# A build-time model of all engines sets the order of the mixing stage; attention's loads one by one

## The chip, the cores and the metric

The kernel runs on one core of a Trainium2 chip. The core has TensorE (PE in the profile, its weight loads PEld), VectorE (DVE), ScalarE (ACT), GpSimd (POOL) and SyncE (SP), which only issues DMA transfers; ACT and POOL issue some as well. Each engine works through its own list of instructions in order and waits for the others by semaphores. The metric is the device time of one execution in microseconds.

## The reference

Two layers (DEPTH 2, width 1024) of a diffusion backbone over 128 context tokens and 512 latent tokens, which share the weights. In each layer:

```
h   = (x * (1 + scale1) + shift1) @ W_in
mix = W_out([ RWKV-7 (4 heads) | neighbourhood attention (4 heads) | GQA (8 q heads, 2 kv heads) ])
x   = LN1(alpha * x + gate1 * mix)
x   = LN2(alpha * x + gate2 * SwiGLU(x * (1 + scale2) + shift2))
```

RWKV is a linear recurrence, forwards and backwards, with a 64 x 64 state per head. In the neighbourhood attention a latent token (8 rows of 64) sees the 8 x 16 tokens around it, with a relative bias, and 256 cached context tokens. In GQA latent tokens see all 512 latent and 256 cached tokens. Context tokens see only each other. All data are fp32; the large products are made of three products of rounded halves.

## The kernel before, in words

A layer runs in stages: the projections with `W_in`, during which the RWKV features begin; `mixing` (L459 on), in which the recurrence and attention run side by side; `mixed`, the first tiles of `W_out`; `tail`, the rest of `W_out`, LN1, the SwiGLU and LN2. Mixing of layer 0 takes about 292 to 562 us of the span, that of layer 1 about 1338 to 1617 us.

The recurrence is done in chunks of 64 tokens, as eight jobs a layer (two pairs of heads, two halves, two directions) in two slots, so that two jobs are under way at a time. A job has these steps. The products FT,BK on PE (two heads and five chunks) give a matrix per chunk; ACT copies it to `X` (L716), and it is written to DRAM as `md` by a DMA that ACT issues (L720) and read back as `BT` in blocks of 16 x 16 by a DMA that POOL issues (L723). DVE inverts the blocks, with some twenty small instructions (L775 to L788). The inverse goes out as `xd` and `td` (L794, L793, issued by ACT) and comes back as `X` and `T` (L799, L797, issued by POOL), two DMAs each, one for each head. Then PE widens the inverse from blocks to chunks, beginning with T times A, and runs through the states S of the five chunks.

Attention is a list of units: six context pairs, then the neighbourhood group 0 (na0) in four units, na1 in four, and four groups of GQA (two kv heads with two halves of the query heads each) in four. A unit makes the scores of two heads on PE into a PSUM tile `ps_s2` (two of them exist), the softmax on DVE and ACT gives `prob`, PE transposes it (PSUM tag `rw`, three banks), and the product with the values goes to `ps_pv`, one bank for a whole group. Names: `qs` and `ks` are queries and keys as they lie for the scores, loaded by SP from DRAM copies (`nqd`, `nkd`, `gqd`, `gkd`); `vw` are the values of a neighbourhood group, eight DMAs from `vd`; `bias` is the relative bias of one head, four DMAs from `rpx` (L948), to which POOL adds a mask (L949). `gv`, `gvc`, `nvc` and `vc` are values of GQA and of the context.

The work is written as Python generators (tasks). Each `yield` gives a latency in us that the author puts for the step. `weave` (L267 to L272) takes the task that is ready first on a clock of its own, `te.now`, which only matmuls move forward. Two attention tasks share the list of units. What the tasks emit isn't the last word: a layer beneath orders each engine's list by priority, which is the order of emission, and by its own simulation, and places the buffers.

```
def weave(self, *tasks):
    while any(t in self.tasks for t in tasks or self.tasks):
        t = min(self.tasks, key=lambda t: (max(t.ready - self.te.now, 0.0), t.ready))
        self.te.now = max(self.te.now, t.ready)
        self.step(t)
```

Of the kernel before, what the change touches and what calls it, by code (L numbers as in the profile page):

```python
# [16 lines left out]
P = 128  # L17
# [12 lines left out]
CH = 64  # L30
# [46 lines left out]


class Task:
    def __init__(self, gen, rank=0):  # L80
        self.gen, self.rank, self.ready = gen, rank, 0.0


class Build:
    def __init__(self, tc, I, O):
        self.tc, self.nc, self.I, self.O = tc, tc.nc, I, O

    def t(self, shape, name, dt=F32):
# [153 lines left out]
    def spawn(self, gen, rank=0):  # L242
        t = Task(gen, rank)
        t.ready = self.te.now
        self.tasks.append(t)
        return t

    def step(self, t):
        lat = next(t.gen, self)
        if lat is self:  # L250
            self.tasks.remove(t)
        else:
            t.ready = self.te.now + (lat or 0.0)

    def tick(self):
# [11 lines left out]
    def weave(self, *tasks):  # L267

        while any(t in self.tasks for t in tasks or self.tasks):
            t = min(self.tasks, key=lambda t: (max(t.ready - self.te.now, 0.0), t.ready))  # L270
            self.te.now = max(self.te.now, t.ready)
            self.step(t)  # L272
# [10 lines left out]
    def psum(self, tag):  # L283

        bufs, n = {"s2": (2, 1024), "rw": (3, 512), "pv": (1, 512)}[tag]
        return self.pp_pool.tile([P, n], F32, name="ps_" + tag, tag="ps_" + tag, bufs=bufs)

# [174 lines left out]
    def mixing(self, l, op):  # L462
        self.op = op
        with self.tc.tile_pool(name=f"at{l}", bufs=2, side="right", reuse_waits="tile") as at:
            self.at = at
            self.load_attn(l)
            for k in range(2, KT):
                self.out[k] = op.tile([P, NT], F32, name=f"o{k}"),
            self.weave(*(self.spawn(self.attention(self.units_), 2) for _ in range(2)))

# [161 lines left out]
    def rwkv_job(self, l, ft, hb, d, slot, pool):  # L632
# [121 lines left out]
        def inverse():  # L754
# [43 lines left out]
            for h in range(2):  # L798
                nc.gpsimd.dma_start(J.X[hs[h]], self.mat(xdr, h))  # L799
            yield 1.5  # L800

# [119 lines left out]
    def load_attn(self, l):  # L921
        nc, I, at = self.nc, self.I, self.at
        self.nvc = at.tile([P, 2, 256], F32, name="nvc", bufs=1)
        nc.gpsimd.dma_start(self.nvc, I["c_na_v"][l])
        self.gvc = at.tile([P, 2, P], F32, name="gvc", bufs=1)
        self.units_ = self.units(l)
        first = next(self.units_)
        self.units_ = itertools.chain([first], self.units_)
        nc.gpsimd.dma_start(self.gvc, I["c_g_v"][l])

    def na_values(self, l, ft):

        nc = self.nc
        vw = self.at.tile([P, 4, 2, P], F32, name="vw", bufs=1)
        vr = self.vd.rearrange("(r c) f -> r c f", c=64)[:, :, ft * P:(ft + 1) * P]
        for j in range(4):
            for hf in range(2):
                nc.sync.dma_start(vw[:, j, hf, :], vr[hf * 4:hf * 4 + 4, NA_LO[j]:NA_LO[j] + NA_N, :])  # L938
        return vw

    def na_bias(self, l, hd):

        nc = self.nc
        bias = self.at.tile([P, 4, 8, NA_N], F32, name="bias", bufs=2)
        for j in range(4):
            b = self.rpx[0:1]
            off = hd * 15 * 16 * (RP - 1) + PAD + 15 + NA_LO[j] - 16 * j
            nc.sync.dma_start(bias[:, j], bass.AP(tensor=b.tensor, offset=b.offset + off, ap=[[RP - 1, P], [16 * (RP - 1), 8], [1, NA_N]]))  # L948
            nc.gpsimd.tensor_tensor(bias[:, j], bias[:, j], bc(self.nmask[:, j * NA_N:(j + 1) * NA_N], 1, 8), ALU.add)  # L949
        return bias  # L950

# [5 lines left out]

    def doubled(self, dram, h):

        t = self.at.tile([P, 2, 768], F32R, name="ks", tag="ks", bufs=3)  # L960
        for u in range(2):
            self.nc.sync.dma_start(self.r32(t[u * CH:(u + 1) * CH]), dram[:, h * CH:(h + 1) * CH, :].rearrange("a p n -> p a n"))
        return t

# [135 lines left out]
    def units(self, l):  # L1100
        def load(ft):
            bias = [self.na_bias(l, 2 * ft + h) for h in range(2)]
            vw, ks = self.na_values(l, ft), [self.doubled(self.nkd[ft], h) for h in range(2)]
            return vw, [(self.stacked(self.nqd[ft], h, "qs", NLAT, 4), ks[h], bias[h]) for h in range(2)]
        vw, qk = load(0)
        for kt in range(6):
            yield self.ctx_pair(l, kt)
        for ft in range(2):
            if ft:
                vw, qk = load(ft)  # L1110
            st = {}
            for j in range(4):
                yield self.na_pair(l, ft, j, qk, vw, st)
        for kv in range(2):
            ks = self.doubled(self.gkd, kv)
            for m in range(2):
                qs = [self.stacked(self.gqd[2 * m + u], kv, "qs", NLAT, 4) for u in range(2)]
                st = {}
                for t in range(4):
                    yield self.gqa_pair(l, kv, m, t, qs, ks, st)  # L1120

# [36 lines left out]
    def ctx_pair(self, l, kt):  # L1158
# [19 lines left out]
        for h in range(2):  # L1178
            pT.append(self.transposed(pr[h], 1))
            yield 0.8728 if h else 0.0  # L1180
        pv = self.psum("pv")
        for h in range(2):
# [11 lines left out]
    def na_pair(self, l, ft, j, qk, vw, st):  # L1194
# [5 lines left out]
        for h in range(2):  # L1200
# [9 lines left out]
            mx = self.tp.tile([P, 1], F32, name="mx", tag="mx", bufs=4)  # L1210
            nc.vector.tensor_tensor_reduce(ps[:, 0:nw], ps[:, 0:nw], bias[:, j].rearrange("p r n -> p (r n)"), 1.0, mc, ALU.add, ALU.max, mx)
            nm = self.tp.tile([P, 1], F32, name="nm", tag="nm", bufs=4)
            nc.vector.tensor_scalar(nm, mx, -1.0, None, ALU.mult)
            if j == h == 0:
                st["sm"] = self.tp.tile([P, 4, 2], F32, name="sms", tag="sms", bufs=2)
            pr.append(self.softmax(ps[:, 0:512], 512, nm, 1.0, st["sm"][:, j, h:h + 1]))
            yield 3.2729999999999997 if h else 0.0
        for h in range(2):
            pT.append(self.transposed(pr[h], 4))
            yield 1.091 if h else 0.0  # L1220
        if j == 0:
            st["pv"] = self.psum("pv")
        pv = st["pv"]
# [4 lines left out]
        if j == 3:  # L1228
# [3 lines left out]
            view = lambda t: t.rearrange("p (j r c) -> p j r c", j=4, r=8)  # L1232
            self.normed(o.rearrange("p (r j c) -> p j r c", r=8, j=4), pv, st["sm"], view)

    def gqa_pair(self, l, kv, m, t, qs, ks, st):
# [4 lines left out]
        for h in range(2):  # L1240
# [8 lines left out]
            nc.vector.tensor_tensor(nm, nm, sc, ALU.mult)  # L1249
            if t == h == 0:  # L1250
                st["sm"] = self.tp.tile([P, 4, 2], F32, name="sms", tag="sms", bufs=2)
            pr.append(self.softmax(ps[:, 0:768], 768, nm, sc, st["sm"][:, t, h:h + 1]))
            yield 3.8185 if h else 0.0
        for h in range(2):
            pT.append(self.transposed(pr[h], 6))
            yield 1.3092 if h else 0.0
        if t == 0:
            st["pv"] = self.psum("pv")
        pv = st["pv"]
# [5 lines left out]
        if t == 3:  # L1265
            yield 1.0
            self.normed(self.out[4 + 2 * kv + m][0][:, NCTX:], pv, st["sm"], lambda t: t)


# [342 lines left out]
```

## Time and profile before

| | us |
|---|---|
| median of 3 runs | 2172.19 (2167.08 to 2173.63) |
| the profiled execution | 2173.96 |
| its span | 2172.2 |
| PE busy | 2056.1 (95%) |
| DVE busy | 1304.0 (60%) |
| ACT busy | 909.6 (42%) |
| POOL busy | 250.5 (12%) |

The mean granted clock of TensorE is 0.967 of full speed. Busy time counts neither the issue of DMAs nor waits. A row of a timeline gives the start and the time of a run of equal instructions; what stands in brackets is the engine's idle time just ahead of it and what ended that. PE's rows name the shape of the part of the array that an instruction uses (128*128, 128*64, 64*128, 64*64) ahead of the tile. PE's small matmuls in fp32 are counted twice by the profile (two passes) and once in the order.

### The profile page before, as it was taken

To read this page: it belongs to the slowest core of one execution; us is meant where nothing else is said; L and a number is where in the kernel's file an instruction comes from. 1 tells how busy PE (TensorE), PEld (TensorE's weight loads), DVE (VectorE), ACT (ScalarE), POOL (GpSimd) and SP (SyncE) were. 2 spreads that over 40 slices of the span, in tenths; PEclk is the share of its full clock that TensorE was granted. 3 is DMA by queue.
4 is the path that set the end of the run, shared out by engine and by line. 5 is a ranking of instruction groups with operands and counts; after the bars stand their busy time and mean duration, and the time that the engine had idled before them with its cause. 6 is when DMAs were issued, how large, how long until landed. Compare 5 with 4: busy or idle time off the path is not lost.

```text
span 2172.2 us, 41222 instructions
## 1 busy us (share of the span) xinstructions
PE 2056.1 (95%) x16737; PEld 1863.3 (86%) x16737; DVE 1304.0 (60%) x2874; ACT 909.6 (42%) x1823; POOL 250.5 (12%) x435
## 2 busy tenths in 40 slices
PE   6989989799999999999999999879999999999997
PEld 4877877577889999999989887657779999999997
DVE  6536677586776666666766567657767533233247
ACT  3434455455563212222466445546555421221234
POOL 0012242121100000000020224311101000000000
PEclk9999998899999999999999999879999999999998
DMA  8555354110414444444431415521114122222223
GB/s 296 147 155 167 108 107 91 41 44 20 153 63 142 150 145 156 146 146 144 142 133 69 134 64 106 99 55 27 32 45 138 61 74 73 72 70 84 77 84 111
DMA packets 158276, 226.48 MB, mean 104 GB/s; under 512 B 88533, under 2 KB 99413, under 8 KB 157957
## 3 DMA queue, kind: packets, MB, share of 16 engines
q1 hardware_dynamic: 118244, 200.82, 29.7%
q0 software_dynamic: 7568, 17.83, 3.0%
q10 hardware_dynamic: 32274, 5.20, 1.4%
q8 instruction: 132, 2.16, 0.4%
q14 instruction: 58, 0.48, 0.1%
HBM read 198.37 MB, written 25.40 MB: 103 GB/s over the span
## 4 chain that ended last, share of the span: by engine, by line
PE 78%; DMA 9%; DVE 5%; ACT 3%; issue 2%; SPq 1%; POOL 0%; ACTq 0%; POOLq 0%; DVEq 0%
PE ps_s L72 44%; PE ps_rw L72 26%; PE ps_pv L72 5%; PE ps_rw L76 4%; DMA td<-TB 2%; DMA qs<-nqd 2%; DMA wmod<-in_w_mod 1%; DMA T<-td 1%; SPq L948 1%; ACT whi L277 0%; DVE wlo L278 0%; SPq L938 0%; DMA xa<-in_xT 0%; DMA c_raw<-in_cT 0%; DMA vw<-vd 0%
## 5 line engine op out<-in xcount | busy, mean ns | idle before, releaser
L72 PE MATMUL ps_s<-xh,whi 128*128 128x320 f32 x1312 | 420.7, 323 | 25.2 <-ACT xh L277 11.6
L72 PE MATMUL ps_s<-xh,wlo 128*128 128x320 f32 x1312 | 412.8, 315 | 2.5 <-DVE wlo L278 2.5
L72 PE MATMUL ps_s<-xl,whi 128*128 128x320 f32 x1312 | 412.6, 315 | 0.6 <-DVE xl L278 0.4
L72 PEld LDWEIGHTS ps_s<-xh,whi 128*128 128x128 f32 x1312 | 251.6, 192 | 48.7 <-ACT xh L277 13.7
L72 PEld LDWEIGHTS ps_s<-xh,wlo 128*128 128x128 f32 x1312 | 252.1, 192 | 7.1 <-DVE wlo L278 4.4
L72 PEld LDWEIGHTS ps_s<-xl,whi 128*128 128x128 f32 x1312 | 252.4, 192 | 5.8 <-issue 2.9
L278 DVE TENSOR_TENSOR wlo<-wraw,whi 128x1024 fp32r<-128x1024 f32 (+1 forms) x118 | 141.3, 1198 | 157.5 <-ACT whi L277 157.1
L72 PE MATMUL ps_s<-xh,flo 128*128 128x320 f32 x736 | 228.4, 310 | 0.0
L72 PE MATMUL ps_s<-xl,fhi 128*128 128x320 f32 x736 | 228.3, 310 | 0.0
L72 PE MATMUL ps_s<-xh,fhi 128*128 128x320 f32 x736 | 228.3, 310 | 0.0
L277 ACT CAST whi<-wraw 128x1024 fp32r<-128x1024 f32 (+1 forms) x118 | 121.2, 1028 | 246.4 <-PE ps_s L72 144.7
L277 ACT CAST fhi<-wraw 128x1024 fp32r<-128x1024 f32 (+1 forms) x82 | 83.3, 1016 | 206.1 <-PE ps_s L72 99.5
L72 PEld LDWEIGHTS ps_s<-xh,fhi 128*128 128x128 f32 x736 | 138.7, 188 | 0.1
L72 PEld LDWEIGHTS ps_s<-xl,fhi 128*128 128x128 f32 x736 | 138.7, 188 | 0.0
L72 PEld LDWEIGHTS ps_s<-xh,flo 128*128 128x128 f32 x736 | 138.6, 188 | 0.1
L278 DVE TENSOR_TENSOR flo<-wraw,fhi 128x1024 fp32r<-128x1024 f32 (+1 forms) x82 | 96.9, 1183 | 57.8 <-ACT fhi L277 57.8
L1431 ACT ACTIVATE sg<-ps_s 128x320 f32<-128x320 f32 x88 | 38.2, 434 | 189.5 <-PE ps_s L72 189.3
L1432 DVE TENSOR_TENSOR sg<-sg,ps_s 128x320 f32<-128x320 f32 x88 | 42.7, 485 | 123.1 <-ACT sg L1431 122.5
L72 PE MATMUL ps_s<-ks,qs 128*128 128x256 f32 (+1 forms) x384 | 101.9, 370 | 11.6 <-DMA qs<-nqd 6.8
L1278 DVE SCALAR_TENSOR_TENSOR z<-ps_rw,modT,z 128x128 f32<-128x128 f32 (+2 forms) x144 | 58.9, 435 | 89.7 <-PE ps_rw L72 89.5
L1287 POOL COPY lnS<-z 128x320 f32<-128x320 f32 x8 | 6.3, 786 | 917.1 <-DVE z L1278 892.6
L72 PE MATMUL ps_rw<-hh,flo 128*128 128x320 f32 x352 | 109.1, 310 | 0.6 <-DVE flo L278 0.6
(400 smaller groups left out, 4642.4 us busy)
## 6 DMA issues: line engine op xcount, KB each, us to landing
wraw<-in_w_ffn_in SPq DMA_DIRECT2D x88, 512.0 KB
wmod<-in_w_modT SPq DMA_DIRECT2D x66, 512.0 KB
wraw<-in_w_in_f SPq DMA_DIRECT2D x42, 512.0 KB
wraw<-in_w_ffn_out SPq DMA_DIRECT2D x48, 448.0 KB
wmod<-in_w_mod SPq DMA_DIRECT2D x48, 256.0 KB
wraw<-in_w_out SPq DMA_DIRECT2D x16, 512.0 KB
wraw<-in_w_ffn_out SPq DMA_DIRECT2D x16, 512.0 KB
ks<-nkd SPq DMA_DIRECT2D x16, 384.0 KB
```

The source lines that it names most:

```text
L72: self.eng.matmul(out, lhsT, rhs, **kw)
L76: self.eng.transpose(out, src, ident)
L277: self.nc.scalar.copy(hi, src)
L278: self.nc.vector.tensor_tensor(lo, src, self.r32(hi), ALU.subtract)
L948: nc.sync.dma_start(bias[:, j], bass.AP(tensor=b.tensor, offset=b.offset + off, ap=[[RP - 1, P], [16 * (RP - 1), 8], [1, NA_N]]))
L1278: nc.vector.scalar_tensor_tensor(z[:, a:b], ps[:, q], g, xa[:, q], ALU.mult, ALU.add)
L1287: nc.gpsimd.tensor_copy(self.lnS[c], z)
L1431: nc.scalar.activation(sg, pg, AF.Silu)
L1432: nc.vector.tensor_tensor(sg, sg, pu, ALU.mult)
```

## The change

`weave` now asks a model of all engines, kept while the program is built. After each step `Model` reads the instructions that were emitted, and puts on each a start after the last writer of what it reads and after its engine, a duration by its kind and size, and, for a matmul whose tile shape isn't that of the matmul ahead, 0.1 us more. Of each task it keeps when its last step is due, and for each place in the code whether the step that stood there began with a matmul, of which shape, and which PSUM tags it took. `weave` takes the task with the earliest start on the model's PE; 0.1 us is added where the tile shape changes, and 0.1 us taken off for the tasks of the recurrence. In mixing PE's list is then fixed to that order (`manual_schedule`); those of the other engines are ordered as before. The latency of the step that loads T and X is 8.0 in place of 1.5.

Attention's loads become a task of their own. Of a neighbourhood group it loads `braw`, one DMA of 128x8x48 for each head in place of four of 128x8x32, which lies in the buffer of `vw`; then `qs` and `ks` of one head and of the other; then POOL makes the eight masked `bias` tiles out of `braw` (eight buffers); then `vw`. The groups come in the order na0, GQA 0.0, GQA 0.1, na1, GQA 1.0, GQA 1.1, and units wait until their group is loaded. Only one group at a time holds `ps_pv`.

```diff
+    def add(self, ins):
...
+            if ins.ins[0].bass_ap.dtype == F32R:
+                d = max(n * 0.458e-3, 0.06)
+            elif ins.is_transpose:
+                d = max(n, m) / 1200
+            else:
+                d = 2 * max(n * 0.883e-3, m / 1200)
+            d *= (mode[0] / 128) * (mode[1] / 128) * (1.25 if mode != (128, 128) else 1.0)
+            if mode != self.mode:
+                d += 0.1
+                self.mode = mode
+            self.pe = max(self.pe, t) + d
+            end = self.pe + 0.15
+        elif op == "DMACopy":
+            issue = {E.SP: 0.5, E.Pool: 0.65, E.Activation: 0.3}.get(e, 0.4)
+            t = self.place(e, t, issue)
+            q = (e, "q")
+            end = self.free[q] = max(self.free.get(q, 0.0), t + 1.3) + outs[0][5] * outs[0][6] * 4 / 200e3
+            end += 0.7
+        else:
+            d = {E.DVE: (0.15, 1.04e-3), E.Activation: (0.14, 0.87e-3), E.Pool: (0.2, 2.4e-3)}.get(e, (0.1, 0.0))
+            end = self.place(e, t, d[0] + n * d[1])
...
+    def start(self, t):
+
+        m = self.model
+        pe, mode, tags = self.known.get(t.at(), (True, None, ()))
+        if not pe:
+            return t.due, t.due
+        s = max(t.due, m.pe)
+        for tag in tags:
+            old = self.ring[tag][-self.banks[tag][0]:]
+            if len(old) == self.banks[tag][0]:
+                s = max(s, max((u[5] for u in m.used.get(old[0], ())), default=0.0))
+        return s + (0.1 if mode and mode != m.mode else 0.0) - (0.1 if t.rank < 2 else 0.0), t.due
...
-            t = min(self.tasks, key=lambda t: (max(t.ready - self.te.now, 0.0), t.ready))
+            t = min(self.tasks, key=self.start)
...
-            self.weave(*(self.spawn(self.attention(self.units_), 2) for _ in range(2)))
+            with self.tc.manual_schedule(engines={mybir.EngineType.PE}):
+                self.weave(*(self.spawn(self.attention(self.units_), 2) for _ in range(2)))
...
-            yield 1.5
+            yield 8.0
...
+        if hd % 2 == 0:
+            self.braw[hd // 2] = self.at.tile([P, 2, 8, 48], F32, name="braw", tag="vw", bufs=1)
+        raw = self.braw[hd // 2][:, hd % 2]
...
+        self.nc.sync.dma_start(raw, bass.AP(tensor=b.tensor, offset=b.offset + off, ap=[[RP - 1, P], [16 * (RP - 1), 8], [1, 48]]))
+
+    def na_masked(self, hd, j):
+        bias = self.bias[hd, j] = self.at.tile([P, 8, NA_N], F32, name="bias", bufs=8)
+        o = NA_LO[j] - 16 * j + 16
+        self.nc.gpsimd.tensor_tensor(bias, self.braw[hd // 2][:, hd % 2, :, o:o + NA_N], bc(self.nmask[:, j * NA_N:(j + 1) * NA_N], 1, 8), ALU.add)
...
+        def na(ft):
+            for h in range(2):
+                self.na_bias(l, 2 * ft + h)
+                yield 1.0
+            for h in range(2):
+                self.qs[ft, h] = self.stacked(self.nqd[ft], h, "qs", NLAT, 4)
+                yield 1.3
+                yield from self.doubled(self.nkd[ft], h, (0, 2 * ft + h))
+            for j in range(4):
+                for h in range(2):
+                    self.na_masked(2 * ft + h, j)
+                yield 1.6
+            yield from self.na_values(l, ft)
...
+        for n, (g, need) in enumerate(((0, ()), (2, ()), (3, (0,)), (1, (0, 2)), (4, (3,)), (5, (1,)))):
+            yield from after(*need)
+            yield from na(g) if g < 2 else gqa((g - 2) // 2, g % 2)
+            self.got.add(g)
...
+        while self.pvs if j == 0 else "pv" not in st:
+            yield 0.5
```

PE's list before, layer 0, in GQA beside a job of the recurrence (`ST`, `A`, `S`, `BK` are its operands):

```order
L72 MATMUL ps_s2_5938<-ks_5400,qs_5891 128x512
L76 MATMUL ps_rw_5928<-ident_78,prob_5768 128x128 x4
L72 MATMUL ps_s2_5938<-ks_5400,qs_5891 128x512
L72 MATMUL ps_s2_5938<-ks_5400,qs_5891 128x256 x2
L72 MATMUL ps_s2_6036<-ks_5400,qs_5889 128x512
L76 MATMUL ps_rw_5934<-ident_78,prob_5768 128x128 x2
L76 MATMUL ps_rw_5956<-ident_78,prob_5821 128x128 x4
L76 MATMUL ps_rw_5962<-ident_78,prob_5821 128x128 x2
L72 MATMUL ps_pv_5617<-pT_5927,gv_2435 64x128
L72 MATMUL ps_s2_6036<-ks_5400,qs_5889 128x512
L72 MATMUL ps_rw_5968<-S0_5966,A10_5794 64x64 x2
L72 MATMUL ps_pv_5617<-pT_5955,gv_2435 64x128
```

PE's list now, in the same part of GQA:

```order
L72 MATMUL ps_s2_5844<-ks_5347,qs_5431 128x512 x2
L72 MATMUL ps_s2_5844<-ks_5347,qs_5431 128x256 x2
L72 MATMUL ps_rw_5856<-S0_5784,A10_5650 64x64 x2
L72 MATMUL ps_rw_5861<-RV1_5521,N1_5407 64x64 x10
L72 MATMUL ps_s2_5873<-ks_5347,qs_5462 128x512 x2
L72 MATMUL ps_s2_5873<-ks_5347,qs_5462 128x256 x2
L72 MATMUL ps_rw_5884<-T1_5695,A01_5516 64x64 x10
L72 MATMUL ps_rw_5896<-S0_5784,A10_5650 64x64 x2
L72 MATMUL ps_s2_5901<-ks_5347,qs_5462 128x512 x2
L72 MATMUL ps_s2_5901<-ks_5347,qs_5462 128x256 x2
L72 MATMUL ps_rw_5911<-N1_5883,X1_5694 64x64 x10
```

The scores of a head stand together now; before, transposes and pieces of the product with the values stood between their halves.

SP's list before, layer 0, from the first load of attention on:

```order
L948 DMA bias_2973<-rpx0_1055 128x8x32 x4
L948 DMA bias_2982<-rpx0_1055 128x8x32 x4
L938 DMA vw_2991<-vd0_2436 128x1x128 x8
L962 DMA ks_3000<-nkd0_1128 64x2x768 x2
L962 DMA ks_3003<-nkd0_1128 64x2x768 x2
L955 DMA qs_3006<-nqd0_1127 128x1x512
L955 DMA qs_3008<-nqd0_1127 128x1x512
```

And now:

```order
L1111 DMA braw_2942<-rpx0_1055 128x8x48 x2
L1154 DMA qs_3007<-nqd0_1127 128x1x512
L1161 DMA ks_3034<-nkd0_1128 64x2x768 x2
L1154 DMA qs_3165<-nqd0_1127 128x1x512
L1161 DMA ks_3182<-nkd0_1128 64x2x768 x2
L1100 DMA vw_3408<-vd0_2414 128x1x128 x8
L1161 DMA ks_3467<-gkd0_1571 64x2x768 x2
```

The first `qs` was the twenty-first load and is the third; `vw` stands behind the keys.

POOL's list before, layer 0, around the masks of na1 and the reads of a job (`A` are the masked products):

```order
L797 DMA T1_3671<-td3_1025 64x5x64 x2
L799 DMA X1_3670<-xd3_1022 64x5x64 x2
L949 TENSOR_TENSOR bias_3935<-bias_3935,nmask_86 128x256 x4
L949 TENSOR_TENSOR bias_3944<-bias_3944,nmask_86 128x256 x3
L726 TENSOR_TENSOR A00_3882<-X0_3721,omask_82 128x320
```

And now:

```order
L1042 COPY S0_4652<-st_1066 128x64
L1116 TENSOR_TENSOR bias_5006<-braw_4727,nmask_86 128x256
L1116 TENSOR_TENSOR bias_5008<-braw_4727,nmask_86 128x256
L1116 TENSOR_TENSOR bias_5021<-braw_4727,nmask_86 128x256
L1116 TENSOR_TENSOR bias_5023<-braw_4727,nmask_86 128x256
L1116 TENSOR_TENSOR bias_5047<-braw_4727,nmask_86 128x256
L1116 TENSOR_TENSOR bias_5049<-braw_4727,nmask_86 128x256
L1116 TENSOR_TENSOR bias_5084<-braw_4727,nmask_86 128x256
L1116 TENSOR_TENSOR bias_5086<-braw_4727,nmask_86 128x256
L961 DMA X0_4116<-xd4_1028 64x5x64
L959 DMA T0_4117<-td4_1031 64x5x64 x2
```

The masks stood behind the reads of a job, and stand ahead of them now.

## Rows read from the trace of the kernel before

**Rows 1.** The page: its span, and busy time by engine.

```profile
span 2172.2 us, 41222 instructions
PE 2056.1 (95%) x16737; PEld 1863.3 (86%) x16737; DVE 1304.0 (60%) x2874; ACT 909.6 (42%) x1823; POOL 250.5 (12%) x435
```

**Rows 2.** Stretches: us, busy PE, PEld, DVE, ACT, POOL (instructions), clock, DMA share, GB/s.

```profile
292.20:562.00 269.80, 243.27 (x2873) 190.50 (x2872) 189.63 (x559) 149.69 (x353) 57.84 (x86) 0.93 0.28 59
420.00:560.00 140.00, 136.82 (x1724) 109.74 (x1722) 105.26 (x279) 82.96 (x175) 24.07 (x34) 1.00 0.12 30
1338.00:1617.00 279.00, 251.41 (x2936) 197.20 (x2932) 190.60 (x561) 147.23 (x347) 58.64 (x89) 0.93 0.26 57
324.00:343.60 19.60, 18.51 (x103) 13.06 (x103) 11.03 (x45) 6.16 (x17) 0.39 (x2) 0.52 0.13 45
```

**Rows 3.** Waits of PE, layer 0's mixing: us in total, times, longest us.

```profile
PE ps_rw L72 <- DMA T<-td: 12.5, 4, 11.6
PE ps_s L72 <- DMA qs<-nqd: 3.9, 1, 3.9
```

**Rows 4.** Waits of PE, layer 1's mixing.

```profile
PE ps_rw L72 <- DMA T<-td: 15.6, 2, 8.5
PE ps_s L72 <- DMA qs<-nqd: 2.9, 1, 2.9
```

**Rows 5.** PE's timeline, three stretches of layer 0: start, us, instruction.

```profile
303.13 0.80 PE L72 MATMUL ps_rw<-N,X 64*64 64x64 f32 x20
303.76 0.75 PE L72 MATMUL ps_rw<-X,N 64*64 64x64 f32 x20
304.44 0.37 PE L72 MATMUL ps_s<-gkc,gqc 64*128 64x128 f32 x1
...
479.60 1.09 PE L72 MATMUL ps_pv<-pT,gv 128*64 128x128 f32 x16
480.52 0.61 PE L72 MATMUL ps_pv<-pT,gvc 128*64 128x128 f32 x8
...
505.46 0.80 PE L72 MATMUL ps_rw<-T,A 64*64 64x64 f32 x20
506.19 0.66 PE L76 MATMUL ps_rw<-ident,prob 128*128 128x128 f32 x4
506.77 0.43 PE L72 MATMUL ps_pv<-pT,gv 128*64 128x128 f32 x2
507.13 0.44 PE L76 MATMUL ps_rw<-ident,prob 128*128 128x128 f32 x2
```

**Rows 6.** SP's timeline, first loads of layer 0.

```profile
290.21 8.32 SPq L948 DMA_DIRECT2D bias<-rpx  x8
308.07 2.50 SPq L955 DMA_DIRECT2D qs<-nqd  x2
```

**Rows 7.** All engines' timeline: a job of layer 1, last products to first T,A.

```profile
1562.62 0.71 PE L72 MATMUL ps_rw<-FT,BK 64*128 64x128 f32 x4
...
1583.26 0.68 DVE L788 TENSOR_REDUCE XB<-tmpB 40x64 f32<-40x512 f32 x1
...
1586.63 0.70 POOL L799 DMA_DIRECT2D X<-xd  x1 [2.95 <-DMA xd<-XB]
...
1590.80 0.33 PE L72 MATMUL ps_rw<-T,A 64*64 64x64 f32 x2
```

**Rows 8.** Timelines of SP, ACT's queue and POOL around a late T.

```profile
439.56 2.24 SPq L955 DMA_DIRECT2D qs<-gqd  x2
...
440.55 0.29 ACTq L793 DMA_DIRECT2D td<-TB  x1
...
451.27 0.69 POOL L797 DMA_DIRECT2D T<-td  x1 [10.86 <-DMA td<-TB]
```

**Rows 9.** Waits of POOL, 285 to 1620 us: total, times, longest.

```profile
POOL X L799 <- DMA xd<-XB: 47.5, 9, 12.9
```

**Rows 10.** The tile bias, POOL's masks: least, median, most ns, first and last start.

```profile
L949 POOL TENSOR_TENSOR bias<-bias,nmask x32: 715/727/1587, 294.3 to 1407.3; 128x256 f32<-128x256 f32 x32
```

## What is expected of the time, and why

> **What bounds the kernel now.** Read the page first. TensorE (PE) is busy 2056.1 of 2172.2 us; VectorE (DVE) stands at 60%, ScalarE at 42% [rows 1]. Only instructions of the two mixing stages are put in a new order, so next I read the windows of those stages. In 292.2 to 562 PE is busy 243.27 of 269.80 us, in 1338 to 1617 it is busy 251.41 of 279.00 [rows 2]: it idles 26.5 + 27.6 = 54 us. In the calm second half of layer 0's stage, 420 to 560, it idles 3.2 us in 140 at clock 1.00 [rows 2]. So the stage is PE's list plus a few waits, and the list's price and those waits are what the change can move.
>
> Then the waits of PE. In each stage two entries carry a DMA: T<-td (12.5 us in 4 waits, one of 11.6; then 15.6 us in 2) and qs<-nqd (3.9; 2.9) [rows 3, 4]. Together 28.1 + 6.8 us of the 54. Last, the clock: both stages show a mean of 0.93 [rows 2]. With two levels, 1.2 and 2.4 GHz (0.5 and 1.0), 0.07 below full over 269.8 us is 38 us at the half level, and 39 us in the other. The row of 324 to 343.6, just behind the qs wait, stands at 0.52 [rows 2]; there PE had idled and came back slow.
>
> **Term 1: PE's list, fewer changes of tile shape.** PE's rows carry the shape that the array is cut into (64*64, 128*64, 128*128). Counted in the order of both kernels, neighbours of different shape are 884 before and 679 after; by stretch (ahead of layer 0's mixing, in it, between, in layer 1's, behind) 192, 289, 92, 308, 3 against 179, 209, 73, 218, 0. That is 205 fewer, with the matmuls the same 13595. What one change costs is in the starts of consecutive rows [rows 5]. Twenty small matmuls 64*64 take 303.76 - 303.13 = 0.63 us when the same shape follows; with 128*128 behind them they take 506.19 - 505.46 = 0.73: 0.10 more. The P times V pieces are 0.0575 us each in a run ((480.52 - 479.60)/16); two alone between 128*128 groups take 507.13 - 506.77 = 0.36 instead of 0.115: 0.25 more. The change from 64*64 to 64*128 shows 0.05 (304.44 - 303.76 = 0.68 against 0.63). I take 0.15, between the two measured kinds that vanish (split score groups and single P times V pieces), with 0.05 and 0.25 as ends: 205 x 0.15 = 31 us, ends 10 and 51. About a tenth of it falls where PE waits for something anyway and isn't saved: -28 us.
>
> The Trainium skill, "TensorEngine Tiling (Array Packing)", section "Key Properties", says that changing the tiling mode drains the engine; the trace agrees that a change costs, 0.10 to 0.25 us. With the fixed part of about 175 ns that "TensorE: Matmul & The Clock Gate" (section "Single matmul latency") gives for a lone matmul, the estimate would be 205 x 0.175 = 36 us, inside the ends above.
>
> **Term 2: the first loads.** Before, SP issues 8 bias loads (8.32 us), then vw and ks, and qs<-nqd goes out at 308.07, 18 us after the first [rows 6]; PE then waits 3.9 us for it, 2.9 in layer 1. After, two loads of 128x8x48 stand where eight of 128x8x32 stood (393 KB for 1049 KB) and the first qs is third in SP's list. At one us each it goes out some 15 us earlier. The wait is covered: -7 us. Nothing worse than the old wait is likely here, as the ctx pairs still come first; ends -7 and +3 (a qs that lands as late as before and PE reaching it 5 us sooner in each stage).
>
> **Term 3: T and X of the recurrence.** Each job has one long latency that PE depends on, and five jobs a layer have it inside mixing: from its last FT,BK matmul over md, BT, the inverse on DVE, td/xd and their read back, to the first T,A. The quickest in the trace runs from 1562.62 to 1590.80: 28.2 us, of which the last 6.9 us, from the end of DVE's inverse at 1583.94, are the way over xd and td [rows 7]. What hides it is the PE work that the list puts between. I priced that work group by group with the spacings of the trace: before 26.6, 30, 30.6, 34.6, 29.5 us in layer 0 and 23.3, 35.8, 31.7, 31.7, 26.4 in layer 1; after 25.8, 22.9, 24.6, 25, 24.3 and 24, 24.6, 27, 28.5, 18.1. The mean cover falls from 30.0 to 24.5 us. The list is now fixed, so nothing behind a late T,A on PE can slip ahead of it: all of PE waits.
>
> Were every chain like the quickest, a job would wait about 28 - 26 plus what ordinary small waits have already added to that cover (PE idles 2% even in 420 to 560, and DVE evictions inside the cover take time that my price leaves out): I put 1 us for each of nine jobs and 7 for the one with 18.1 us of cover, 16 in all. On top come the hits. A T read at 451.27 waited 10.86 us for its td write, which went out at 440.55 just after SP had issued two qs<-gqd at 439.56 [rows 8]. POOL waits for xd 47.5 us in 9 jobs, 5.3 each, one of 12.9 [rows 9], where the quickest needs 2.95 [rows 7]. The twelve qs loads of a layer remain, only further apart; I count 4 hits of 6 us, 24. Sum 40 us, against 28.1 now: +12. Ends: 10 us in all (every chain covered, -18) and 90 (a rival below).
>
> The Trainium skill speaks against such hits: "DMA: Bandwidth & Descriptors", section "Issuing engines are not separate DMA queues", says that transfers of different issuers interleave on the same engines. Here a td write issued 1 us behind two qs loads landed over 10 us late, so the trace differs. By the page the four hits would be gone and the sum 24 us lower.
>
> **Term 4: POOL.** The eight masks of the second neighbourhood group were spread and stood behind a T/X read; in the new list of layer 0 they stand together just ahead of the X and T reads of a job. Each takes 0.73 us [rows 10], 5.8 together, and the first waits for braw, which waits for the last use of vw. X and T are released late by up to 6 us if the masks are; I take +2, ends 0 and 12.
>
> **Term 5: the clock.** It falls behind a stall that lasts some us. The qs stall goes, and one or two long T waits stay or are replaced by other ones, so I take 0 on balance; ends -20 (about half of the 77 us at half speed regained, halved) and +15.
>
> The recurrence's work that moves into mixing (some 5 us a layer) leaves the projections, where PE never waits for long: 0.
>
> **Sum.** -28 - 7 + 12 + 2 + 0 = -21. The profiled execution took 2173.96 us, which gives 2153. It stands 1.8 above the median of 2172.19, so 2151.2; I say 2152. With only the middle of the ends together the forecast's own range is 2130 to 2167.
>
> **Rivals.**
>
> First, slower: T late at every job. The covers are priced, the quickest chain is 28.2 us, and the mean seen is nearer 33 (28.2, plus 2 to 3 for xd above the quickest, plus BT and DVE queueing of the same size). 33 - 24.5 = 8.5 us a job, for ten jobs 85 to 90 us against 28.1: +60; the clock falls behind each such stall: +5 to 10. -28 - 7 + 60 + 8 = +33: 2205. It decides from the point where the mean wait of a job exceeds 6 us (60 - 28 = 32 eats terms 1 and 2). For it: the cover did fall by 5.5 us, and PE can't run ahead. Against: chains shorten when DVE meets them less loaded, and evictions inside the cover stretch it. Chance 0.22.
>
> Second, no change: PE's saved time becomes waiting. The recurrence is a chain of jobs in two slots; if its latencies, not PE, set the stage's length, a cheaper list only idles more. For it: the T,A of successive jobs stand some 45 us of PE work apart before and 31 after, so the jobs follow at their latency. Against: in 420 to 560 PE idles 3.2 us [rows 2]. -28 - 7 + 35 = 0: 2172. Chance 0.17.
>
> Third, a larger gain: the loads one by one no longer hit any td write, the T waits shrink to 10 us, and the clock stays up. 205 x 0.19 = 39, -7, -18, -12: -76, 2096 to 2098. For it: the 16 bias loads of a stage become four, and no burst of eight stands ahead of a td write any more. Against: the same qs loads remain. Chance 0.14.
>
> That the list isn't really PE's order is no rival: the rows of PE show whole score groups and runs of transposes where single ones alternated.
>
> **How the numbers follow.** Forecast 0.47, slower rival 0.22, no change 0.17, larger gain 0.14. The range that should hold 8 in 10 goes from 2112 (most of the larger gain is left out) to 2196 (half of the slower case). What a measurement of this kernel can't tell from no change is 0.3%, 6.5 us: 2165.7 to 2178.7. Faster: nearly all of the forecast (0.44), the larger gain (0.14) and a little of the second rival (0.03), 0.61. Same: 0.12 of the second rival, 0.03 of the forecast and 0.02 of the first, 0.17. Slower: 0.20 of the first and 0.02 of the second, 0.22.
>
> **What would show it.** Term 1: PE's busy time falls by about 25 to 30 us, nearly all of it inside the two mixing stages. Term 2: no wait for qs<-nqd at the first neighbourhood unit. Term 3: waits T<-td in most jobs, 1 to 8 us each, 40 in all; above 60 the first rival has it, under 15 the third. Term 4: X and T reads of a job of layer 0 issued right behind eight masks. Term 5: stage clocks of 0.92 to 0.94; 0.97 or more speaks for the third rival. If PE's busy time falls and the idle time rises by as much with the same T waits, it is the second. The forecast is wrong if a change of shape costs under 0.08 us, or if one new wait, such as that for vw behind the masks, is worth over 15 us.

## The result

The changed kernel is slower: 2242.3 us, median of 4 runs (2235.9 to 2246.0), against 2172.5; the ratio is 1.0323 with a 95% interval of 1.0291 to 1.0355. The forecast was 2152 and its range ended at 2196. The profiled execution has a span of 2234.1 us, 61.9 more than before.

The page of the changed kernel, span and busy time by engine (they answer to [rows 1]):

```profile
span 2234.1 us, 41206 instructions
PE 2044.0 (91%) x16737; PEld 1868.1 (84%) x16737; DVE 1302.1 (58%) x2874; ACT 914.8 (41%) x1826; POOL 244.1 (11%) x435
```

PE's busy time fell by 12.1 us, so its idle time rose by 74.0. The two mixing stages, from the first context score to the first matmul of `W_out` (columns as in [rows 2]):

```profile
287.90:600.50 312.60, 244.60 (x2971) 197.95 (x2970) 197.21 (x577) 154.91 (x362) 61.09 (x92) 0.90 0.20 47
1363.10:1684.20 321.10, 260.60 (x3093) 209.69 (x3091) 207.72 (x610) 162.75 (x377) 63.71 (x98) 0.88 0.20 47
```

PE idles 68.0 and 60.5 us in them, where it idled 26.5 and 27.6 in the stretches of [rows 2]. The granted clock of the whole span fell from 0.967 to 0.954; with two levels, 1.2 and 2.4 GHz, that is 205 us at the half level where there were 143. The waits of PE, layer 0 and then layer 1 (they answer to [rows 3, 4]):

```profile
PE ps_rw L72 <- DMA T<-td: 13.9, 3, 12.7
PE ps_s L72 <- ACT prob L1323: 9.7, 6, 3.3
PE ps_rw L72 <- DVE X L992: 5.4, 1, 5.4
PE ps_rw L76 <- ACT A L1024: 5.2, 1, 5.2
PE ps_rw L76 <- DVE N L880: 4.3, 3, 2.9
...
PE ps_s L72 <- ACT prob L1323: 14.5, 11, 2.5
PE ps_rw L76 <- DVE RV L906: 8.0, 2, 7.6
PE ps_rw L72 <- DMA T<-td: 5.3, 2, 5.1
```

No qs<-nqd is left, and T<-td takes 19.2 us against 28.1. What is new are many waits for ACT and DVE. Added up over all lines of this view, ACT and DVE, they are 25.4 + 22.4 us in layer 0 and 24.2 + 25.5 in layer 1, 97.5 in all; before, 18.5 (the expectations below say 95 and 19). Many are for a PSUM bank: scores wait until ACT has read the last scores of that bank (`ACT prob`), and the transposes of `prob` often wait for an instruction that makes none of their operands (`DVE N`, `ACT A`) but reads a bank of `ps_rw`. For the rest the view doesn't tell a late operand from a bank that is still to be read.

One such wait in the timeline of all engines of the changed kernel, layer 1 (start, time, instruction, in brackets the idle time ahead of it):

```profile
1425.80 1.22 PE L72 MATMUL ps_s<-ks,qs 128*128 128x256 f32 x4
...
1427.48 0.22 DVE L1055 TENSOR_TENSOR S<-T,ps_rw 128x64 f32<-128x64 f32 x1
...
1427.62 0.48 DVE L1409 CUSTOM_DVE_ANT_0 ps_s<-ps_s,bias,mc 128x256 f32<-128x256 f32 x1
...
1428.23 0.14 DVE L1411 TENSOR_SCALAR nm<-mx 128x1 f32<-128x1 f32 x1
...
1428.46 0.69 ACT L1323 ACTIVATE prob<-ps_s,nm 128x512 f32<-128x512 f32 x1 [2.13 <-DVE nm L1411]
...
1429.30 1.22 PE L72 MATMUL ps_s<-ks,qs 128*128 128x256 f32 x4 [1.46 <-ACT prob L1323]
...
1430.45 0.48 PE L72 MATMUL ps_rw<-S,A 64*64 64x64 f32 x4
```

From the start of the scores to the freed bank it takes 3.5 us. The list has the next scores in that place, so PE stands still 1.46 us, though a piece of the recurrence, S times A, comes right behind, and DVE had written its `S` by 1427.70.

And the longest wait, at the start of layer 0's stage:

```profile
286.61 0.52 SPq L1154 DMA_DIRECT2D qs<-nqd  x1
...
286.70 0.28 ACTq L956 DMA_DIRECT2D xd<-XB  x1
...
287.34 0.98 ACTq L955 DMA_DIRECT2D td<-TB  x1
...
302.26 0.73 POOL L961 DMA_DIRECT2D X<-xd  x1 [11.57 <-DMA xd<-XB]
...
310.27 1.34 POOL L959 DMA_DIRECT2D T<-td  x2 [7.28 <-DMA td<-TB]
...
312.92 0.34 PE L72 MATMUL ps_rw<-T,A 64*64 64x64 f32 x1 [12.70 <-DMA T<-td]
```

The first loads of attention go out earlier, as the change has it, and now stand just ahead of a job's `xd` and `td`: POOL can load X only 15.6 us after `xd` was issued. It looks like the collision of [rows 8] at another place; e7 below tests that. The clock of 300 to 320 is 0.58.

### The profile page after: what moved, and what is told of

It is laid out like the page before. It is cut to its first block, busy times and chain, and to the rows that moved or that the text cites. A ratio compares the mean times of both kernels' runs of the same rounds, so it can differ in the third digit from the quotient of the medians.

```text
span 2234.1 us, 41206 instructions
## 1 busy us (share of the span) xinstructions
PE 2044.0 (91%) x16737; PEld 1868.1 (84%) x16737; DVE 1302.1 (58%) x2874; ACT 914.8 (41%) x1826; POOL 244.1 (11%) x435
## 5 line engine op out<-in xcount | busy, mean ns | idle before, releaser
L76 PE MATMUL ps_rw<-ident,prob 128*128 128x128 f32 x536 | 95.1, 310 | 27.7 <-DVE N L880 5.6
L72 PE MATMUL ps_s<-ks,qs 128*128 128x256 f32 (+1 forms) x384 | 92.4, 366 | 24.3 <-ACT prob L1323 24.1
L72 PE MATMUL ps_rw<-hh,wlo 128*128 128x320 f32 x352 | 108.8, 309 | 1.3 <-DVE wlo L433 1.3
```

The lines of the kernel that those rows point to most:

```text
L72: self.eng.matmul(out, lhsT, rhs, **kw)
L76: self.eng.transpose(out, src, ident)
```

## The experiments

The change has three parts: the loads one by one, the choice of tasks by the model, and the fixed list. A fourth thing came up in the traces, the form of the qs loads. Medians in us, with the ratio to the runs of before on the same chip (before: 2170 to 2173 throughout). "One by one" stands for all that the loads brought along: the new order of the groups, `braw` in the buffer of `vw`, one holder of `ps_pv`, and the step of 8.0 us for T and X. Of those rows only e11 has that step at 1.5 us:

| loads | qs DMA | weave's choice | PE's list | us | ratio, 95% | run |
|---|---|---|---|---|---|---|
| old | whole | old | free | 2172 | 1 | before |
| old | whole | old | fixed | 2186.7 | 1.0055 to 1.0105 | e2 |
| one by one | whole | old | free | 2174.0 | 1.0002 to 1.0042 | e3 |
| one by one | whole | old | fixed | 2231.6 | 1.0232 to 1.0300 | e6 |
| one by one | whole | model | free | 2204.4 | 1.0119 to 1.0216 | e1 |
| one by one | whole | model | fixed | 2242.3 | 1.0291 to 1.0355 | after |
| old | halves | old | free | 2130.2 | 0.9770 to 0.9834 | e8 |
| old | halves | old | fixed | 2173.9 | 0.9993 to 1.0023 | e13 |
| one by one | halves | old | free | 2165.6 | 0.9956 to 1.0005 | e11 |
| one by one | halves | model | free | 2163.9 | 0.9945 to 0.9991 | e10 |
| one by one | halves | model | fixed | 2207.4 | 1.0115 to 1.0203 | e7 |

### e1 to e4: which part it is

e1, the list free again (e2 puts the same line into the kernel before; e4 adds DVE and ACT to its set of engines):

```diff
-            with self.tc.manual_schedule(engines={mybir.EngineType.PE}):
-                self.weave(...)
+            self.weave(...)
```

> The changed kernel, but PE's list in mixing is not fixed: the layer beneath orders it again. Theory F (the fixed list makes PE wait for evictions of ACT and DVE, 95 us of such waits in the two stages after against 19 before): those waits fall back to 20 to 35 us and the time to 2165 to 2185, with changes of tile shape at 825 instead of 679. Theory M (the order in which the model emits tasks is bad by itself) and theory L (the loads one by one and the single holder of ps_pv delay attention): the time stays at 2220 to 2245.

> The kernel before, with nothing changed but that PE's list in mixing is fixed to the order of emission (774 changes of tile shape instead of 884). Theory F: the waits of PE for ACT and DVE rise by 40 us or more and the time to 2200 to 2245. Theories M and L: nothing that makes the change slow is in it, 2150 to 2175, the lower end by the changes of shape saved (110 x 0.15 = 16 us).

e3, beside the free list:

```diff
-            t = min(self.tasks, key=self.start)
+            t = min(self.tasks, key=lambda t: (max(t.ready - self.te.now, 0.0), t.ready))
```

> The loads one by one, the order of the groups and the 8.0 us alone: weave picks by the old key and PE's list is free. Theory F: 2165 to 2185, like the kernel before. Theory M: the same, 2165 to 2180. Theory L: 2215 to 2245.

> The changed kernel with the lists of DVE and ACT fixed to the order of emission too, beside PE's. If PE waits because DVE and ACT work in another order than the one that PE's list was made for (F1), the waits for ACT and DVE fall from 95 us to under 50 and the time to 2180 to 2215. If PE waits because the model's durations are too short and a fixed list can't give way (F2), it stays at 2235 or rises to 2270, since DVE and ACT can no longer give way either. Theories M and L: 2235 to 2250.

Measured 2204.4, 2186.7, 2174.0 and 2364.2 us. Theory F (the fixed list) holds in part: freeing the list gives back 38 us, and fixing it alone costs 16, both less than expected; the loads alone cost 3. Theory M (the model's choice of tasks) holds for 30 us, the step from e3 to e1. These 38, 30 and 3 make up the 70 us. Theory L (the loads) falls on this evidence (but see e11). F1, that DVE and ACT only work in another order than PE's list was made for, falls clearly: with DVE and ACT in the order of emission the kernel loses 122 us more. The groups of PE's instructions that wait, over the whole kernel (instructions, busy us and mean ns, idle us ahead of them and what ended it): the kernel before, e2, the scores in e1, the changed kernel.

```profile
L72 PE MATMUL ps_s<-ks,qs 128*128 128x256 f32 (+1 forms) x384 | 101.9, 370 | 11.6 <-DMA qs<-nqd 6.8 <-ACT prob L1127 4.7
L76 PE MATMUL ps_rw<-ident,prob 128*128 128x128 f32 x536 | 89.6, 294 | 1.9 <-DVE RV L838 0.8 <-ACT prob L1127 0.4 <-ACT X L716 0.4
```

```profile
L76 PE MATMUL ps_rw<-ident,prob 128*128 128x128 f32 x536 | 93.8, 308 | 13.3 <-ACT T L853 6.6 <-ACT pT L1156 2.3 <-DVE N L719 1.2
L72 PE MATMUL ps_s<-ks,qs 128*128 128x256 f32 (+1 forms) x384 | 89.9, 359 | 20.1 <-ACT prob L1128 20.1
```

```profile
L72 PE MATMUL ps_s<-ks,qs 128*128 128x256 f32 (+1 forms) x384 | 101.9, 372 | 9.0 <-ACT prob L1322 8.9
```

```profile
L76 PE MATMUL ps_rw<-ident,prob 128*128 128x128 f32 x536 | 95.1, 310 | 27.7 <-DVE N L880 5.6 <-ACT A L1024 5.2 <-ACT X L878 2.5
L72 PE MATMUL ps_s<-ks,qs 128*128 128x256 f32 (+1 forms) x384 | 92.4, 366 | 24.3 <-ACT prob L1323 24.1
```

Fixing the list makes the scores' wait for `prob` four times as long with the old emission (4.7 to 20.1) and not quite three times with the model's (8.9 to 24.1). All waits of PE for ACT and DVE, over the whole profiled execution, are 60 us before, 77 in e3, 95 in e1 and 144 in the changed kernel: of the 84 us more, the fixed list brings 49, the model's choice 18 and the loads 17. In e2 the T<-td waits fell from 28.1 to 5.7 us at the same time, which hides most of its price.

### e5, e6 and e9: is it the model?

e5:

```diff
-        t = max([...]) + 0.07
+        t = max([...]) + 0.2
-            end = self.free[q] = max(self.free.get(q, 0.0), t + 1.3) + ...
+            end = self.free[q] = max(self.free.get(q, 0.0), t + 3.0) + ...
-            end = self.place(e, t, d[0] + n * d[1])
+            end = self.place(e, t, 1.4 * (d[0] + n * d[1]))
```

> The changed kernel with longer prices in the model: 1.4 times the duration of every DVE, ACT and POOL instruction, 0.2 us in place of 0.07 from one engine to the next, 3.0 in place of 1.3 us to start a DMA. Changes of tile shape stay at 681. If PE waits because the model's prices are too short, so that the fixed list asks for results before they are there: waits of PE for ACT and DVE, 95 us in the two stages, fall under 60, and the time to 2195 to 2220. If any fixed list does this, since DVE and ACT work in an order that the model doesn't know: 2230 to 2255, with waits as before.

e6 is e3 with the list fixed again.

> The changed kernel with weave's old key; PE's list stays fixed, the loads stay one by one (746 changes of tile shape). If the two parts add (fixing +16 on the old emission, the model's choice of tasks +30, the loads +3): 2185 to 2200. If the model's choice is only slow where the list is fixed to it, the same; if the loads one by one are what a fixed list stumbles on: 2215 to 2245.

e9:

```diff
             if mode != self.mode:
-                d += 0.1
                 self.mode = mode
...
-        return s + (0.1 if mode and mode != m.mode else 0.0) - (0.1 if t.rank < 2 else 0.0), t.due
+        return s - (0.1 if t.rank < 2 else 0.0), t.due
```

> The changed kernel, PE's list fixed, but a change of tile shape costs nothing in the model (723 changes instead of 679). If it is the grouping that makes PE wait (runs of score groups and of transposes that need PSUM banks faster than ACT and DVE empty them): the waits before the transposes of prob (27.7 us) and before the scores of ks,qs (24.3 us) fall by a third or more, and the time to 2205 to 2230. If any fixed list waits like this, however it is grouped: 2240 to 2255, the upper part by the 44 changes more.

Measured 2233.7, 2231.6 and 2261.5 us. Longer prices gave 9 us where 20 to 45 were expected, and the two intervals overlap, so short prices aren't the main thing, as far as one other set of prices can tell. Dropping the price of a shape undid a part of the grouping (44 more changes of the 205 saved). It shortened the waits ahead of the transposes from 27.7 to 19.4 us and ahead of the scores from 24.3 to 21.9, but the time got worse by 19 us: so far as it was undone, grouping isn't what costs the time. And e6 shows that the model's choice matters little once the list is fixed (11 us); the expected sum of parts, 2185 to 2200, was wrong, since loads and fixing together cost 60 us and apart 3 and 16.

### e7, e8, e10, e11 and e14: the loads of qs

In e7, e8, e10 and e11 each qs load goes out as two DMAs:

```diff
-        self.nc.sync.dma_start(self.r32(t), dram[:, h * CH:(h + 1) * CH, :])
+        for u in range(2):
+            self.nc.sync.dma_start(self.r32(t[u * CH:(u + 1) * CH]), dram[u, h * CH:(h + 1) * CH, :])
```

> The changed kernel with each qs load issued as two DMAs of 64x512, one for each half of the partitions, in place of one of 128x1x512; PE's list keeps its order row for row. If qs loads block the writes of xd, td and md issued behind them: the waits of PE for T<-td (19 us) fall under 8, the 7.6 us for RV at the start of layer 1's mixing goes, and the time falls to 2205 to 2225. If those hits come from the braw loads (1024 pieces of 192 bytes each) or from POOL's masks: 2235 to 2250, with the 12.7 us wait of layer 0 still there.

> The kernel before, with each qs load as two DMAs of 64x512. If qs loads block the writes of the recurrence: the 28.1 us of T<-td waits fall under 10, the clock of the stages rises, and the time is 2135 to 2155. If they don't: 2168 to 2175.

> The changed kernel with PE's list free and each qs load as two DMAs of 64x512. Before with the same loads takes 2130. If the model's choice of tasks costs its 30 us because it moves loads and writes of the recurrence against each other: 2130 to 2145. If it costs them by the order of the work itself: 2155 to 2175.

> A version of the best parts: the loads one by one with each qs as two DMAs, weave by the old key, PE's list free, and the T/X step at 1.5 us again. If the first loads (2 braw in place of 8 bias) save the wait for the first scores and the clock behind it: 2115 to 2128, below the 2130 of before with qs in halves. If the loads one by one bring nothing or cost some us as they did with whole qs loads (+3.5): 2130 to 2140.

e14 is e8 with this:

```diff
-            bias = [self.na_bias(l, 2 * ft + h) for h in range(2)]
-            vw, ks = self.na_values(l, ft), [self.doubled(self.nkd[ft], h) for h in range(2)]
-            return vw, [(self.stacked(self.nqd[ft], h, "qs", NLAT, 4), ks[h], bias[h]) for h in range(2)]
+            qk = [(self.stacked(self.nqd[ft], h, "qs", NLAT, 4), self.doubled(self.nkd[ft], h)) for h in range(2)]
+            bias = [self.na_bias(l, 2 * ft + h) for h in range(2)]
+            return self.na_values(l, ft), [(q, k, b) for (q, k), b in zip(qk, bias)]
```

> The kernel before with qs in halves, and of a neighbourhood group qs and ks are loaded ahead of bias and vw. If the wait for the first scores (the idle 4.8 us in 320 to 340 and the half clock behind it, in both layers) came from qs standing behind eight bias and eight vw loads: 2112 to 2126. If bias is then what is late: 2126 to 2140.

Measured 2207.4 (e7), 2130.2 (e8), 2163.9 (e10), 2165.6 (e11) and 2124.8 us (e14, ratio 0.9785, 0.9760 to 0.9809). The collision is shown by e7, whose PE list is the changed kernel's row for row and which takes 35 us less. Its timeline of POOL at the place of the longest wait:

```profile
294.40 0.73 POOL L961 DMA_DIRECT2D X<-xd  x1 [2.73 <-DMA xd<-XB]
297.18 1.34 POOL L959 DMA_DIRECT2D T<-td  x2 [2.05 <-DMA td<-TB]
```

11.57 us have become 2.73 and 7.28 have become 2.05, and T<-td is no longer among PE's waits, there or anywhere in e7; the same braw loads stand ahead as before, so they weren't the cause. (Only the first of the two qs loads stands ahead of `xd` here, as the halves take SP longer to issue; what the whole load does to the DMA engines is shown in the last section.) In the kernel before, the halves take the T<-td waits from 28.1 to 1.1 us and 41 us from the time. The two mixing stages of e8:

```profile
292.40:542.70 250.30, 234.92 (x2874) 185.47 (x2873) 189.29 (x560) 149.70 (x353) 57.52 (x86) 0.97 0.31 64
1315.70:1579.30 263.60, 252.24 (x2975) 197.09 (x2974) 194.90 (x574) 151.33 (x361) 61.23 (x94) 0.95 0.30 62
```

Idle 15.4 and 11.4 us, clock 0.97 and 0.95 for 0.93. So a good part of the clock's loss went together with these waits.

By its time e10 falls under the second of its readings (2155 to 2175), the order of the work itself. Set beside e11 it reads otherwise: the same loads with the old key take 2165.6, so the model's choice costs nothing there, and the halves gave some 40 us with the model's choice (e1 to e10) and only 8 with the old key (e3 to e11). So the model's 30 us were collisions; but e11 also has the step of 1.5 us where e10 has 8.0, and no run separates the two. What keeps both at 2165 is in e11: the loads one by one cost 35 us against e8, where e3 had shown 3. With whole qs loads they avoid collisions (T<-td and qs waits are 14.2 us in e3, 34.9 before), which fits a gain there that hides most of the cost. In e11's span PE idles 21 us more than in e8's, 19 of them as waits for ACT and DVE (82.5 against 63.7), and some 40 us more are at the half clock; which of the loads' pieces does it (the order of the groups, the masks in a row, the shared buffer of `vw` and `braw`, the one holder of `ps_pv`) was not settled.

e14 is the fastest kernel run, 2.2% below before. Its 5 us against e8 aren't told apart for sure: the intervals of the two ratios overlap.

### e13: the fixed list without collisions

e8 with PE's list fixed as in e2.

> The kernel before with qs in halves (2130 us) and PE's list in mixing fixed to the order of emission (774 changes of tile shape instead of 880). At 0.14 us a change the list is 15 us cheaper. If a fixed list only loses where DMA hits make results late: 2112 to 2130. If it loses by waiting for ACT and DVE at PSUM banks, whatever the loads do: 2138 to 2165, with waits for ACT and DVE at 35 us or more above those with the list free (63.7 us in the whole kernel).

Measured 2173.9: fixing costs 44 us against e8, more than expected, although the list has 106 changes of shape less. In the mixing stages the waits for ACT and DVE are 59.9 us against 23.2. The largest in layer 0 of e13:

```profile
PE ps_s L72 <- ACT prob L1129: 11.4, 7, 2.3
PE ps_rw L72 <- DVE S L894: 4.3, 7, 1.4
PE ps_s L72 <- ACT prob L1132: 4.3, 4, 1.8
```

No DMA is among them; layer 1 has 1.8 us of T<-td. So the price of fixing is in the list itself: 44, 44 (e7 against e10), 38 and 57 us, and 16 only in e2, where T<-td fell by 22 us.

### e12: what a change of shape costs

```diff
+            for x, y in ((a, t), (c, t), (a, c)):
+                for n in (20, 1, 2, 5):
+                    for _ in range(20 // n):
+                        for f in (x, y):
+                            for _ in range(n):
+                                f()
```

> The kernel before with matmuls on the identity added behind layer 0, PE's list fixed there: pairs of 64*64 and 128*128, of 128*64 and 128*128, of 64*64 and 128*64, each 20 and 20 in a row, then alternating singly, in twos and in fives. What one change of shape costs is (alternating minus in a row) over 39, 19 and 7 changes less. By the rows of before: 0.05 to 0.25 us each, 0.10 for 64*64 to 128*128 and 0.2 for 128*64 to 128*128. If it is under 0.08 us, term 1 was too large and the changed kernel never had 28 us to gain; at 0.15 or more term 1 stands and the waits ate it.

PE's timeline in e12: twenty in a row and then single ones; further on twos and fives.

```profile
1148.10 2.54 PE L72 MATMUL ps_pv<-ident 64*64 64x64 f32 x40
1150.57 2.40 PE L76 MATMUL ps_pv<-ident 128*128 128x128 f32 x20
1152.90 0.32 PE L72 MATMUL ps_pv<-ident 64*64 64x64 f32 x2
1153.15 0.33 PE L76 MATMUL ps_pv<-ident 128*128 128x128 f32 x1
1153.41 0.32 PE L72 MATMUL ps_pv<-ident 64*64 64x64 f32 x2
...
1213.22 0.65 PE L72 MATMUL ps_pv<-ident 128*64 128x128 f32 x4
1213.80 0.44 PE L76 MATMUL ps_pv<-ident 128*128 128x128 f32 x2
1214.17 0.65 PE L72 MATMUL ps_pv<-ident 128*64 128x128 f32 x4
...
1222.78 1.31 PE L72 MATMUL ps_pv<-ident 128*64 128x128 f32 x10
1224.02 0.76 PE L76 MATMUL ps_pv<-ident 128*128 128x128 f32 x5
1224.71 1.31 PE L72 MATMUL ps_pv<-ident 128*64 128x128 f32 x10
```

In a row a pair of 64*64 and 128*128 takes (2.47 + 2.33) / 20 = 0.240 us; alternating, 1153.41 - 1152.90 = 0.51 with two changes: 0.135 each. For 128*64 and 128*128, two pairs with two changes take 0.95 us and five with two changes 1.93, so a pair takes 0.327 and a change 0.148. The third kind, 64*64 with 128*64, comes out at 0.14 in the same way. All three readings are from stretches at clock 1.00.

## Why the prediction was wrong

**The step that failed most** is in term 3: "The list is now fixed, so nothing behind a late T,A on PE can slip ahead of it". That holds for every late operand and every PSUM bank, and I drew it for T,A alone. All other waits I left as they were ("PE idles 2% even in 420 to 560"), which puts a fixed list's price at nothing without a reason. With the list free the changed kernel gets back 38 us (e1), and the fixed list is 49 of the 84 us by which PE's waits for ACT and DVE rose. It needs no mistake of the model: the old emission, fixed, has such waits too, 65.5 us in the two stages of e2 and 59.9 in e13, where the free list has 18.5 and 23.2, and longer prices (e5) hardly changed the time.

**The second step** is the hits: four of 6 us in term 3, and term 2's sentence "Nothing worse than the old wait is likely here". The wait for qs went, but the loads that I had moved forward were not followed to what stands behind them: `xd` and `td` of a running job. At the start of layer 0 that made the 12.7 us wait, and e7 takes it away. In layer 1 a wait of 7.6 us for RV stands at the same place, 3.8 at most in e7. The prediction has no term for what the model's choice of tasks does to such collisions; it cost 30 us (e1 against e3), and whole qs loads cost the changed kernel 35 us (e7). These 35 are partly the same 30, so they don't add.

**Term 1** was right in price and number: 205 x 0.14 = 29 us, by e12. It doesn't show whole in PE's busy time (-12.1 us). That 62 us more ran at the half clock explains it, by an estimate: from e8 to e13 106 changes went, 15 us, and 54 us more ran at the half level, and PE's busy time stayed (+0.8), so a us at the half level adds about 0.29 us; 62 of them add 18, and -29 + 18 = -11. The Trainium skill ("TensorEngine Tiling (Array Packing)", "Key Properties") says that a change of mode drains the engine. The trace agrees that a change costs, 0.14 us; that a drain is what costs it no run here shows.

**Term 3** in itself was too large: T<-td 19.2 us in place of 40. The shorter cover (24.5 us for 30) was enough for most jobs; where it was not, a load had hit, as e7, which has no such wait left, shows. The first rival, T late at every job, forecast a slower kernel but by a mechanism that isn't there; that its 2205 lies on the right side is luck.

**Term 4** was right in size. POOL's and PE's timelines of the changed kernel, layer 0, where the masks of na1 stand ahead of a job's reads:

```profile
405.53 4.84 POOL L1116 TENSOR_TENSOR bias<-braw,nmask 128x256 f32<-128x256 f32 x7 [0.84 <-DMA braw<-rpx]
410.31 0.69 POOL L961 DMA_DIRECT2D X<-xd  x1
410.99 1.34 POOL L959 DMA_DIRECT2D T<-td  x2
...
416.90 0.79 PE L72 MATMUL ps_rw<-T,A 64*64 64x64 f32 x18 [1.00 <-DMA T<-td]
```

X and T go out right behind the masks, and PE waits 1.0 us for T in this place.

**Term 5** was taken as 0, with stage clocks of 0.92 to 0.94. With more stalls the clock fell to 0.90 and 0.88 in the stages; by the estimate above that cost some 18 us of busy time, beyond the end of +15.

That mixing could gain most in another place was in [rows 8]: the late td behind two qs loads was read as a hit of 6 us that would happen four times. Those loads cost the kernel before 41 us (e8).

The prediction also took [rows 8] to differ from transfers that interleave. They do interleave there, as the last section shows; the load ahead is slow.

Open are the 35 us of the loads one by one once qs is in halves, and why fixing costs 57 us in e6 and 44 in e13.

## What to carry to other kernels

A fixed order on an engine turns every error of the plan into a stall of all that stands behind, so weigh its gain (here 29 us of fewer changes of shape) against all waits for operands and for PSUM banks, not only against the one that is long today. When a load moves forward, look at which other transfers are issued just behind it. And when a small write lands 10 us late, look at the DMA share beside it, and try the form of the load ahead of it first: two lines gave 41 us here.

## What was not expected of the hardware

One qs load as a single DMA of 128x1x512 held up transfers that another engine issued behind it by 5 to 9 us (waits of 11.57 against 2.73 and 7.28 against 2.05 us); the same bytes as two DMAs of 64x512 did not. The whole load is slow in itself. The rows are [rows 8]'s stretch in the kernel before, the wait at the start of layer 0 in the changed kernel, and two halves in e8 (columns as in [rows 2]):

```profile
445.00:452.00 7.00, 7.00 (x78) 5.37 (x75) 4.44 (x11) 4.59 (x10) 0.69 (x1) 1.00 0.14 49
```

```profile
300.00:303.00 3.00, 0.22 (x2) 0.03 (x1) 1.48 (x5) 1.24 (x5) 0.73 (x1) 1.00 0.14 49
```

```profile
460.00:462.00 2.00, 2.00 (x38) 1.83 (x36) 2.00 (x5) 0.91 (x3) 0.00 (x0) 1.00 0.53 131
```

A share of 0.14 of 16 DMA engines is little more than two of them at work, at 49 GB/s, for as long as the load lasts; the two halves move the same 256 KB at 131 GB/s and are done in 2 us. Why a whole load uses so few engines no run here tests; its two halves are the outer dimension of its address pattern, and e7's edit takes that dimension away. In 445 to 452 the trace has, in each us, 23 packets of 2048 bytes from SP's queue and 21 to 25 of 64 bytes from ACT's: the small write takes turns with the load, packet by packet, on the few engines that the load holds. The Trainium skill ("DMA: Bandwidth & Descriptors", "Issuing engines are not separate DMA queues") has transfers of different issuers interleave on the same engines; the trace agrees, by these counts.

The clock fell in e12 while PE was busy without a gap, in the stretch of small matmuls of 64*64 and 128*128 that change shape after each one, two or five (the first 4 us of it still at 1.00):

```profile
1148.00:1157.00 9.00, 9.00 (x86) 7.18 (x84) 6.15 (x11) 3.60 (x5) 0.72 (x9) 1.00 0.17 61
1157.00:1185.00 28.00, 28.00 (x137) 18.64 (x136) 0.00 (x0) 0.00 (x0) 0.00 (x0) 0.51 0.00 1
```

PE is shown as busy for 28 of 28 us at 0.51, so idle time in PE's records is not the only thing ahead of a fall. Nor does every such stretch bring it about: 128*64 and 128*128 in turn ran at 1.00 from 1197 to 1209.
